# Four waits of a hand-made merge of TensorE's threads, held longer

## The chip, the core and the metric

The program runs on one core of a Trainium2 chip. That core has five engines with a queue of instructions each, worked off in program order: TensorE (PE, with its weight loads listed as PEld), VectorE (DVE), ScalarE (ACT), GpSimd (POOL) and SyncE (SP), which starts most transfers. The metric is the time of one launch on the device in microseconds (us), lower is better.

## The reference

Two blocks of a language model run one after the other over 256 tokens with 16 learned ones ahead (T = 272 columns, 1024 channels). All is float32; the kernel splits each matmul operand into a high and a low part (h, l) and adds three products. The first layer of the first block is a gated delta rule:

```python
proj = h @ w_in                                    # queries, keys, values, z, beta, a
qkv  = silu(conv4(proj[..., :o1]))
beta = sigmoid(proj[..., o2:o3])
g    = -exp(a_log) * softplus(proj[..., o3:] + dt_bias)
q, k = l2_normalize(q), l2_normalize(k)            # per head and token
# per head and chunk of 128 tokens: G = cumsum(g); A = 1 + beta k k^T decay (lower);
# u, w = solve(A, [v beta, k beta exp(G)]); v_new = u - w S; o = q exp(G) S + attn v_new; S = S exp(G_end) + k^T v_new
out  = (rms_norm(o) * silu(z)) @ w_out
```

Behind it come a convolutional feed-forward, an mLSTM layer (queries, keys, values, an output gate, and per head and token two gates whose cumulated log sigmoid weights a 272 x 272 attention), another feed-forward, and the second block (feed-forward, three mixing branches, feed-forward), which the change does not touch.

## The kernel before, in words

TensorE's order is fixed when the program is written; the other engines are ordered by a scheduler that works from it. A small merger, the class Threads, keeps a list of generators ("threads"). Each yields what its next piece on TensorE waits for: tiles, names of PSUM banks, and a number, the *hold*, which is added to the time at which the merger believes the tiles are ready. The merger keeps an estimated clock of TensorE and takes the first thread in its list whose time has come; where none has, it takes the one that comes first and moves its clock up. A hold thus puts no wait into the program: it keeps a thread back, and other threads' pieces are written ahead of it.

In the first layer (`gdn`, names below) the threads are:

- `projections`: four groups of queries, keys, values (`gdn_proj`), and eight slices of z (`gdn_z`). They are matmuls `ps<-xhl,wh` and `ps<-xhl,wl`, always in triples of three matmuls of 272 columns. This thread is last in the list and always ready but for the loads, so its triples are what is put between the pieces of the others: the *filler* below.
- `gdn_gates`: `psba`, `bap`, then the chain of a log sigmoid in tiles `lp` to `gg`, then **`gp`** (sums over time, from `gg`), then the tile `stk`, then `rp` (transposes of `stk`), which gives `rw`. Nothing of a head starts before `rw`.
- `first_chunks`, `second_chunks`: `unit_kq` transposes keys and queries (`kqp<-eye,kv`), scales them to unit length in `kqtok`, and transposes back (**`kqp<-eye,kqtok`**); `gdn_pre` builds the decays (`dp`, `kk`). `second_chunks` also runs `after`, with `gdn_onorm`, which scales the outputs `on` and transposes them (**`otp`**), four times for each of four groups, and then `gdn_tail_pre`.
- four lanes (`gdn_core`): an inverse by doubling (`rtp`, then `yp` and `w` in turn, `zp`, `r2p`), then `up`, `op`, `sp`, `ksp`. Lane 0 ends with `gdn_tail`, the last 16 tokens of all heads: the same inverse, `wp`, `up`, `vnp`, `up`, `rsp`. The product with `w_out` (`ps<-og`) comes after all of it.

In the mLSTM layer `ml_gates` does what `gdn_gates` does: a chain on VectorE to `mlf`, then **`mbp`**, then `mst`, then `mrp`; the filler there is again the projection, and the heads (`ml_head`) wait for `mrp`. The four waits in bold type are those of the change.

Loads: each weight slice of 512 KB is loaded to `wraw` (three buffers), cast by ScalarE to `wh`, and subtracted by GpSimd to `wl` (three buffers each). A slice of the projections serves eight triples.

Of the kernel before, what the change touches and what calls it, by code (L numbers as in the profile page):

```python
# [208 lines left out]
class Kern:  # L209
# [681 lines left out]
    def gdn_gates(self, X):  # L891
        i = self.i
        al, db = self.al, self.db
        self.lane = "u0"
        p = self.plane("psba", (128, T))
        yield from self.row_product(i["gdn_w_in"][0], 6144, 32, X, p)
        ba = self.cst([128, 3, 32], name="ba")
        self.V.memset(ba[:], 0.0)
        gr = self.p_s.tile([32, T], F32, tag="th", name="gr", bufs=2)
        self.A.copy(gr[:], p[:32])  # L900
        yield [gr[:], "pu0"]
        self.lane = "u0"
        p = self.plane("bap", (128, 3, 32))
        for t, (o, P) in enumerate(TT):
            self.tr(p[:P, t, :], gr[:, o:o + P], 32)
        for t, (o, P) in enumerate(TT):
            self.V.tensor_copy(ba[:P, t, :], p[:P, t, :])
        bx, ax = ba[:, :, 0:16], ba[:, :, 16:32]
        self.tt(ax, ax, db[:, None, :].to_broadcast([128, 3, 16]), ALU.add)
        l = self.log1p_exp_neg_abs([128, 3, 32], ba[:])  # L910
        self.act(al[:], al[:], AF.Exp)
        g = self.cst([128, 3, 16], name="gg")
        lb = self.cst([128, 3, 16], name="lb")
        self.stt(g[:], ax, 0.0, l[:, :, 16:32], ALU.max, ALU.add)
        self.stt(g[:], g[:], -1.0, al[:, None, :].to_broadcast([128, 3, 16]), ALU.mult, ALU.mult)
        self.stt(lb[:], bx, 0.0, l[:, :, 0:16], ALU.min, ALU.subtract)
        yield [g[:], "pu0", 1.0]
        self.lane = "u0"
        gp = self.plane("gp", (128, 5, 16))
        for t, (o, P) in enumerate(TT):  # L920
            self.mm(gp[:P, t, :], self.tri[:P, :P], g[:P, t, :])
        for t in range(2):
            self.mm(gp[:, 3 + t, :], self.ones[:], g[:, t, :])
        G = self.cst([128, 3, 16], name="Gc")
        self.V.memset(G[:], 0.0)
        for t, (o, P) in enumerate(TT):
            self.V.tensor_copy(G[:P, t, :], gp[:P, t, :])
        self.nG = self.cst([128, 2, 16], name="nG", tag="ba")
        self.ts(self.nG[:], G[:, 0:2, :], -1.0, ALU.mult)
        self.beta = self.cst([128, 3, 16], name="beta")  # L930
        self.act(self.beta[:], lb[:], AF.Exp)
        self.ts(self.beta[:], self.beta[:], 0.5, ALU.mult)
        Pq = self.cst([128, 3, 16], name="Pq")
        self.tt(Pq[:], G[:], lb[:], ALU.add)
        self.ckt = self.cst([128, 2, 16], name="ckt")
        self.tt(self.ckt[:], gp[:, 3:5, :], G[:, 0:2, :], ALU.subtract)
        self.act(self.ckt[:], self.ckt[:], AF.Exp)
        self.cbg = self.cst([128, 16], name="cbg")
        self.act(self.cbg[:], Pq[:, 1, :], AF.Exp)
        self.ts(self.cbg[:], self.cbg[:], -1.0, ALU.mult)  # L940
        self.eg = self.cst([128, 16], name="eg")
        self.act(self.eg[:], G[:, 1, :], AF.Exp)
        self.gt = self.cst([128, 16], name="gt")
        self.act(self.gt[:], gp[:, 4, :], AF.Exp)
        st = self.cst([128, 3, 96], name="stk")
        hi = self.cst([128, 3, 16], F32R, name="sthi")
        for n, (src, sgn) in enumerate(((Pq, 1.0), (G, 1.0), (G, -1.0))):
            if n < 2:
                self.A.copy(hi[:], src[:])
                self.V.tensor_copy(st[:, :, n * 32:n * 32 + 16], hi[:].bitcast(F32))  # L950
                self.tt(st[:, :, n * 32 + 16:n * 32 + 32], src[:], hi[:].bitcast(F32), ALU.subtract)
        self.ts(st[:, :, 64:96], st[:, :, 32:64], -1.0, ALU.mult)
        yield [st[:], "pu0"]
        self.lane = "u0"
        rp = self.plane("rp", (96, T))
        for t, (o, P) in enumerate(TT):
            self.tr(rp[:, o:o + P], st[:P, t, :], P)
        self.rw = self.cst([96, T], F32R, name="rw")
        self.A.copy(self.rw[:], rp[:])
        xs = self.cst([96, 2, 8, 16], F32R, name="xs")  # L960
        self.tt(xs[:], self.rw[:, None, None, 256:272].bitcast(F32).to_broadcast([96, 2, 8, 16]),
                self.c[:96, CSM:CSM + 16].rearrange("p (e q) -> p e q", e=2)[:, :, :, None].to_broadcast([96, 2, 8, 16]),
                ALU.mult)
        self.xs = xs
# [30 lines left out]
    def unit_kq(self, x, c):  # L995


        n = len(x)
        yield list(x) + [f"pu{c}"]
        self.lane = f"u{c}"  # L1000
        ss = self.tiny([128, n], "kqss")
        p = self.plane("kqp", (128, n, 128))
        for h in range(n):
            self.tr(p[:, h, :], x[h])
        for h in range(n):
            self.square_sum(ss[:, h:h + 1], p[:, h, :])
        r = self.rsqrt_small([128, n], ss[:], 1.0, 4 * EPS)
        rq = r[:].rearrange("p (h e) -> p h e", e=2)[:, :, 1]
        self.ts(rq, rq, 128.0 ** -0.5, ALU.mult)
        kq = self.ring(f"kq{c}", "kqtok", (128, n, 128))  # L1010
        for h in range(n):
            self.act(kq[:, h, :], p[:, h, :], AF.Copy, scale=r[:, h:h + 1])
        yield [kq[:], f"pu{c}", 0.8]
        self.lane = f"u{c}"
        p2 = self.plane("kqp2", (128, n, 128))
        for h in range(n):
            self.tr(p2[:, h, :], kq[:, h, :])
        kqT = self.ring(f"kqT{c}", "kqT", (128, n, 128))
        self.A.copy(kqT[:], p2[:])
        return kq, kqT  # L1020
# [179 lines left out]
    def gdn_onorm(self, on, r, dst):  # L1200

        for h in range(2):
            self.ts(on[:, h, :], on[:, h, :], r[:, h:h + 1], ALU.mult)
        yield [on[:], "pu1", 0.5]
        self.lane = "u1"
        p = self.plane("otp")
        for h in range(2):
            self.tr(p[:, h, :], on[:, h, :])
        self.A.copy(dst, p[:])
# [297 lines left out]
    def ml_gates(self, X, done):  # L1507
# [21 lines left out]
        l = self.log1p_exp_neg_abs([128, 3, 4], ga[:, :, 4:8])  # L1529
        lf = self.cst([128, 3, 4], name="mlf", tag="gg")  # L1530
        self.stt(lf[:], ga[:, :, 4:8], 0.0, l[:], ALU.min, ALU.subtract)
        yield [lf[:], "pb1"]
        bp = self.bank("pb1", (128, 3, 3, 4), "mbp")
        st = self.cst([128, 3, 24], name="mst", tag="stk")
        bs = self.cst([128, 3, 3, 4], name="mbs", tag="lb")
# [915 lines left out]
```

## Time and profile before

| | |
|---|---|
| time, median of 3 runs | 1661.56 us (1658.22 to 1662.08) |
| profiled execution, its own time | 1655.78 us |
| its span, first to last instruction | 1654.0 us |
| TensorE busy | 1547.4 us (94%) |
| VectorE busy | 1124.6 us (68%) |
| ScalarE busy | 929.0 us (56%) |
| GpSimd busy | 581.0 us (35%) |
| mean granted TensorE clock | 0.977 of full |

The table averages over stages with different limits. The first layer runs from about 20 to 366 us of the span and the mLSTM layer from about 655 to 771 us.

### The profile page before, as it was taken

The page shows a single profiled execution, that of the slowest core. Times are in us where ns is not written, and L with a number is a line of the kernel's source. Part 1 is how long each engine was busy: PE and PEld are TensorE (multiplying, and loading weights), DVE is VectorE, ACT ScalarE, POOL GpSimd, SP SyncE. Part 2 cuts the span into 40 slices and gives each one's busy share as a digit, 9 for nine tenths or more (in the row PEclk, how much of TensorE's full clock was granted, in tenths as well). Part 3 has the DMA queues.
Part 4 walks back from the last instruction along what each step waited for, and adds up shares of the span by engine and source line. Part 5 has one row for each costly group of instructions (what it writes and reads, how often), then busy time and mean ns, then how long its engine had stood idle before and what let it go on. Part 6 is the DMA issues. An engine that isn't in the chain of part 4 may idle for free.

```text
span 1654.0 us, 31168 instructions
## 1 busy us (share of the span) xinstructions
PE 1547.4 (94%) x11932; PEld 1461.7 (88%) x11932; DVE 1124.6 (68%) x2231; ACT 929.0 (56%) x1885; POOL 581.0 (35%) x535
## 2 busy tenths in 40 slices
PE   7889888899899999899899999999997899999999
PEld 5778777789799998888799999999986899999987
DVE  6788877757888857357877758665659653566643
ACT  4567667656566645445566645554554664564442
POOL 3674555320200000551143533312265548511221
PEclk9899999999999999999999999999998999999999
DMA  5331221226365553344356665665553435656664
GB/s 160 91 90 52 77 60 45 77 90 196 108 186 187 178 176 112 105 116 133 110 179 190 187 182 156 206 193 176 174 166 106 128 90 156 182 160 192 183 187 153
DMA packets 239099, 235.39 MB, mean 142 GB/s; under 512 B 11510, under 2 KB 226406, under 8 KB 238950
## 3 DMA queue, kind: packets, MB, share of 16 engines
q1 hardware_dynamic: 238326, 231.86, 46.7%
q8 instruction: 94, 1.54, 0.4%
q0 software_dynamic: 496, 1.41, 0.4%
q14 instruction: 55, 0.45, 0.1%
q10 hardware_dynamic: 128, 0.13, 0.0%
HBM read 232.32 MB, written 1.05 MB: 141 GB/s over the span
## 4 chain that ended last, share of the span: by engine, by line
PE 68%; DVE 22%; ACT 5%; DMA 3%; issue 2%; POOL 0%; SPq 0%; ACTq 0%; DVEq 0%; POOLq 0%
PE ps L190 53%; PE pst L190 4%; DVE cy L190 3%; DVE rq_a L190 3%; DVE RT L190 2%; ACT wh L190 2%; DVE wl L190 1%; DVE rq_y L190 1%; DVE xn L190 1%; PE rsp L190 1%; DVE xhl L190 1%; DMA wraw<-in_ffn_w_up_dram 1%; DVE on L190 1%; PE w L190 1%; PE up L190 1%
## 5 line engine op out<-in xcount | busy, mean ns | idle before, releaser
L190 PE MATMUL ps<-xhl,wh 128*128 128x256 f32 (+2 forms) x4496 | 859.6, 293 | 28.2 <-DVE py L190 7.4
L190 PEld LDWEIGHTS ps<-xhl,wh 128*128 128x128 f32 x4496 | 701.4, 192 | 37.9 <-DVE xhl L190 8.0
L190 ACT CAST wh<-wraw 128x1024 fp32r<-128x1024 f32 (+2 forms) x436 | 448.1, 1029 | 382.0 <-PE ps L190 255.7
L190 PE MATMUL ps<-xhl,wl 128*128 128x256 f32 (+2 forms) x2248 | 625.5, 287 | 0.0
L383 POOL TENSOR_TENSOR wl<-wraw,wh 128x512 fp32r<-128x512 f32 (+3 forms) x264 | 336.1, 1297 | 645.1 <-ACT wh L190 597.2
L190 PEld LDWEIGHTS ps<-xhl,wl 128*128 128x128 f32 x2248 | 423.6, 192 | 0.0
L190 DVE TENSOR_TENSOR wl<-wraw,wh 128x1024 fp32r<-128x1024 f32 (+2 forms) x237 | 285.7, 1206 | 166.1 <-ACT wh L190 161.5
L190 POOL TENSOR_TENSOR wl<-wraw,wh 128x512 fp32r<-128x512 f32 x134 | 174.5, 1324 | 150.9 <-ACT wh L190 134.1
L190 PE MATMUL ps<-hh,wh 128*128 128x256 f32 (+1 forms) x1056 | 191.1, 283 | 0.0
L190 PEld LDWEIGHTS ps<-hh,wh 128*128 128x128 f32 x1056 | 163.2, 189 | 0.0
L190 PE MATMUL ps<-hh,wl 128*128 128x256 f32 (+1 forms) x528 | 149.8, 284 | 0.0
L190 DVE SCALAR_TENSOR_TENSOR fy<-ps,pvt,fy 128x256 f32<-128x256 f32 (+2 forms) x176 | 84.9, 488 | 25.7 <-ACT fy L190 23.8
L190 PEld LDWEIGHTS ps<-hh,wl 128*128 128x128 f32 x528 | 99.4, 188 | 0.2 <-DVE wl L190 0.2
L190 DVE SCALAR_TENSOR_TENSOR cy<-cx,pvt,cy 128x271 f32<-128x271 f32 (+2 forms) x96 | 74.4, 778 | 13.7 <-ACT cy L190 12.7
L190 DVE TENSOR_TENSOR hh<-fy,hh 128x256 fp32r<-128x256 f32 (+1 forms) x88 | 66.3, 755 | 14.0 <-ACT hh L190 13.9
L190 POOL MEMSET mvt<- 128x4 f32 x4 | 0.4, 102 | 176.1 <-PE ps L190 176.1
L190 DVE TENSOR_TENSOR py<-ps,rstd 128x256 f32<-128x256 f32 x72 | 30.1, 421 | 38.0 <-PE ps L190 38.0
L190 ACT ACTIVATE fy<-ps,pvt 128x272 f32<-128x272 f32 (+1 forms) x88 | 49.6, 568 | 10.8 <-PE ps L190 10.2
L190 PE MATMUL pst<-wh,hh 128*128 128x512 f32 x176 | 55.1, 394 | 0.0
L190 ACT CAST hh<-fy 128x256 fp32r<-128x256 f32 (+1 forms) x88 | 35.7, 407 | 29.0 <-DVE fy L190 28.4
L190 PE MATMUL ps<-og,wh 128*128 128x272 f32 x256 | 49.5, 291 | 0.1
L190 DVE CAST_PREDICATED RT<-lvl,w 128x512 f16<-128x512 uint8 x67 | 44.9, 684 | 6.7 <-PE w L190 6.3
(521 smaller groups left out, 2400.6 us busy)
## 6 DMA issues: line engine op xcount, KB each, us to landing
wraw<-in_ffn_w_up_dram SPq DMA_DIRECT2D x88, 512.0 KB
wraw<-in_ffn_w_gu_dram SPq DMA_DIRECT2D x88, 512.0 KB
wraw<-in_ffn_w_down_dram SPq DMA_DIRECT2D x79, 512.0 KB
wraw<-in_gdn_w_in_dram SPq DMA_DIRECT2D x48, 512.0 KB
wraw<-in_w_in_dram SPq DMA_DIRECT2D x41, 512.0 KB
wraw<-in_ml_w_in_dram SPq DMA_DIRECT2D x24, 512.0 KB
wraw<-in_gdn_w_out_dram SPq DMA_DIRECT2D x16, 512.0 KB
wraw<-in_mem_w_kv_dram SPq DMA_DIRECT2D x8, 512.0 KB
```

The lines of the kernel that those rows point to most:

```text
L190: r = f(*args, **kw)
L383: eng.tensor_tensor(l[:, a, b], r[:, a, b], h[:, a, b].bitcast(F32), ALU.subtract)
```

## The change

Four numbers: the hold of `gp` goes from 1.0 to 5.0, that of `kqp<-eye,kqtok` from 0.8 to 2.5, that of `otp` from 0.5 to 2.5, and `mbp`, which had none, gets 4.0. No instruction's work changes.

```diff
@@ gdn_gates
         self.stt(lb[:], bx, 0.0, l[:, :, 0:16], ALU.min, ALU.subtract)
-        yield [g[:], "pu0", 1.0]
+        yield [g[:], "pu0", 5.0]
         self.lane = "u0"
         gp = self.plane("gp", (128, 5, 16))
@@ unit_kq
             self.act(kq[:, h, :], p[:, h, :], AF.Copy, scale=r[:, h:h + 1])
-        yield [kq[:], f"pu{c}", 0.8]
+        yield [kq[:], f"pu{c}", 2.5]
         self.lane = f"u{c}"
@@ gdn_onorm
             self.ts(on[:, h, :], on[:, h, :], r[:, h:h + 1], ALU.mult)
-        yield [on[:], "pu1", 0.5]
+        yield [on[:], "pu1", 2.5]
         self.lane = "u1"
@@ ml_gates
         self.stt(lf[:], ga[:, :, 4:8], 0.0, l[:], ALU.min, ALU.subtract)
-        yield [lf[:], "pb1"]
+        yield [lf[:], "pb1", 4.0]
         bp = self.bank("pb1", (128, 3, 3, 4), "mbp")
```

Written anew from the first of them on, TensorE's order differs in the whole first layer and in the mLSTM layer, and nowhere else; SyncE's is the same throughout.

On TensorE, at the gates of the first layer, ahead of `gp` (`trx` are transposes of the residual), the difference begins:

```order
 L190 MATMUL ps<-xhl,wl 128x272
+L190 MATMUL ps<-xhl,wh 128x272 x2
+L190 MATMUL ps<-xhl,wl 128x272
+L190 MATMUL trx<-eye,xt 128x128 x2
+L190 MATMUL trx<-eye,xt 128x16
+L190 MATMUL ps<-xhl,wh 128x272 x2
```

and goes on so: ten triples and three `trx` are put in ahead of `gp`, so that 38 triples of filler come before it, where there were 28. Between `gp` and `rp` stood nine triples and three `trx`; now there are eight triples.

On ScalarE, the same place in the program, from `beta` (the last thing ahead of `gp`'s results) on; before:

```order
L190 ACTIVATE beta<-lb 128x48
L190 ACTIVATE eg<-Gc 128x16
L190 COPY hst<-trx 128x272
L190 ACTIVATE cth<-cy 128x272
L190 ACTIVATE ckt<-ckt 128x32
L190 ACTIVATE gt<-gp 128x16
L190 ACTIVATE cbg<-Pq 128x16
L190 CAST sthi<-Pq 128x48
L190 CAST wh<-wraw 128x1024
```

and now:

```order
L190 ACTIVATE beta<-lb 128x48
L190 CAST wh<-wraw 128x1024
L190 COPY cx<-ps 128x272
L190 ACTIVATE cy<-ps,pvt 128x272
L190 COPY hst<-trx 128x272
L190 ACTIVATE cth<-cy 128x272
L190 COPY hst<-trx 128x272
L190 ACTIVATE cth<-cy 128x272
L190 ACTIVATE eg<-Gc 128x16
L190 CAST wh<-wraw 128x1024
L190 ACTIVATE ckt<-ckt 128x32
L190 ACTIVATE gt<-gp 128x16
```

`sthi` holds the high parts from which `stk`, and so `rp`, is made. Two casts of weights and the copies of a projection moved ahead of it.

On TensorE, the end of the first layer; before, filler stood between all steps of `gdn_tail`, as here, and 16 triples behind its last, `rsp`:

```order
L190 MATMUL ps<-xhl,wl 128x272
L190 MATMUL otp<-eye,on 128x128 x2
L190 MATMUL rsp<-sq,ones 128x256
L190 MATMUL ps<-xhl,wh 128x272 x2
L190 MATMUL ps<-xhl,wl 128x272
```

and now the last steps read:

```order
L190 MATMUL r2p<-RT,Z 128x128
L190 MATMUL wp<-R_5253,kbg 128x128 x2
L190 MATMUL otp<-eye,on 128x128 x2
L190 MATMUL up<-R_5253,bv 128x128 x2
L190 MATMUL up<-wq,St 128x2x16 x16
L190 MATMUL vnp<-eye,vnT 128x128 x2
L190 MATMUL otp<-eye,on 128x128 x2
L190 MATMUL up<-BA,vn 128x128 x2
L190 MATMUL rsp<-sq,ones 128x256
L190 MATMUL ps<-og,wh 128x272 x2
```

The filler has moved up: from the start of lane 0's last inverse (its `rtp`) to `ps<-og` there were 63 triples, now 20, and none of them is behind that inverse's last `yp`. In the mLSTM layer 28 triples now stand between `mgp`, the transposes ahead of the gates' chain, and `mbp`, where there were 16, and eight instead of six between `mbp` and `mrp`.

## Rows read from the trace of the kernel before

**Rows 1.** By stretch: length; busy PE, PEld, DVE, ACT, POOL; clock; transfers' share, GB/s.
```profile
20.00:366.00 346.00, 296.42 (x2447) 270.89 (x2448) 264.68 (x631) 220.50 (x663) 180.99 (x196) 0.95 0.26 75
655.00:771.00 116.00, 107.38 (x775) 95.68 (x773) 64.08 (x173) 53.45 (x121) 55.74 (x46) 0.97 0.39 111
```
**Rows 2.** What TensorE waited for from 20 to 380: us in total, times, longest.
```profile
PE yp L190 <- DVE RT L190: 14.4, 11, 3.3
PE kqp L190 <- ACT kqtok L190: 6.7, 4, 3.5
PE gp L190 <- DVE gg L190: 5.3, 1, 5.3
PE otp L190 <- DVE on L190: 5.0, 3, 4.4
...
PE ps L190 <- DVE zs L190: 3.8, 3, 2.0
```

**Rows 3.** TensorE in order of time, around `gp` (start, us, idle before).
```profile
32.37 0.41 PE L190 MATMUL ps<-xhl,wh 128*128 128x272 f32 x2
...
32.75 0.42 PE L190 MATMUL ps<-xhl,wh 128*128 128x272 f32 x2
...
41.05 1.20 PE L190 MATMUL gp<-gg,cc 128*128 128x16 f32 x6 [5.32 <-DVE gg L190]
...
45.51 0.65 PE L190 MATMUL ps<-xhl,wh 128*128 128x272 f32 x2
...
46.19 0.65 PE L190 MATMUL ps<-xhl,wh 128*128 128x272 f32 x2
...
51.52 0.54 PE L190 MATMUL rp<-eye,stk 128*96 128x128 f32 x3 [0.46 <-DVE stk L190]
```

**Rows 4.** TensorE in order of time, at the longest waits of `kqp` and `otp`.
```profile
77.43 1.12 PE L190 MATMUL kqp<-eye,kqtok 128*128 128x128 f32 x4 [3.54 <-ACT kqtok L190]
...
195.48 0.66 PE L190 MATMUL kqp<-eye,kqtok 128*128 128x128 f32 x4 [1.77 <-ACT kqtok L190]
...
234.77 0.69 PE L190 MATMUL otp<-eye,on 128*128 128x128 f32 x2 [4.36 <-DVE on L190]
```

**Rows 5.** The same columns for the stretches behind four of these waits.
```profile
41.00:50.00 9.00, 8.95 (x40) 7.97 (x40) 4.14 (x18) 3.63 (x13) 1.96 (x2) 0.54 0.23 61
...
77.00:83.00 6.00, 5.57 (x23) 4.98 (x24) 4.88 (x8) 4.92 (x15) 3.62 (x3) 0.50 0.07 7
...
234.00:240.00 6.00, 5.23 (x30) 4.73 (x31) 4.51 (x15) 1.84 (x5) 1.52 (x2) 0.50 0.29 87
...
674.00:681.00 7.00, 7.00 (x41) 6.60 (x41) 2.29 (x17) 1.27 (x2) 0.00 (x0) 0.52 0.21 71
```

**Rows 6.** The mLSTM gates in order of time, TensorE and VectorE.
```profile
673.82 0.59 PE L190 MATMUL mbp<-mlf,cc 128*128 128x4 f32 x2 [4.98 <-DVE mlf L190]
...
680.55 0.55 PE L190 MATMUL mrp<-eye,mst 128*24 128x128 f32 x3
...
677.23 0.17 DVE L190 TENSOR_TENSOR mst<-mbs,mhi 128x36 f32<-128x36 f32 x1
```

**Rows 7.** ScalarE's cast for `stk`, and GpSimd's queue at `mrp`.
```profile
48.80 0.25 ACT L190 CAST sthi<-Gc 128x48 fp32r<-128x48 f32 x1
...
681.41 0.74 POOL L190 DMA_DIRECT2D qkw<-in_mla_q_norm_dram  x1 [8.90 <-PE mrp L190]
682.17 2.54 POOL L190 TENSOR_TENSOR wl<-wraw,wh 128x512 fp32r<-128x512 f32 x2
```

**Rows 8.** TensorE in order of time, the end of the first layer.
```profile
332.61 0.28 PE L190 MATMUL yp<-RT,Br 128*128 128x128 f16 x2
...
334.30 0.28 PE L190 MATMUL w<-Y,RT 128*128 128x128 f16 x2
...
358.98 0.60 PE L190 MATMUL rsp<-sq,ones 128*128 128x256 f32 x2
...
366.20 0.56 PE L190 MATMUL ps<-og,wh 128*128 128x272 f32 x2
```

## The prediction

> **What bounds the kernel now.** I read four views. The stretches give the layer: from 20 to 366 TensorE is busy 296.4 of 346 us, so it stands still for 50 us; in the mLSTM layer for 8.6 of 116; VectorE is busy 76% of the first layer [rows 1]. TensorE is therefore what sets the time, wherever it waits for nothing, and the change can only move its idle time and its clock. The list of waits says for whom it waits: 14.4 us in the inverse (`yp` for `RT`), which the change does not name, and 6.7, 5.3 and 5.0 us at `kqp`, `gp` and `otp` [rows 2]. In order of time one sees that `gp`'s is one wait of 5.32 us [rows 3], that the largest at `kqp` are 3.54 and 1.77 us and one of 4.36 us makes up `otp`'s [rows 4], and that `mbp` waits 4.98 us [rows 6]. These 22 us are the places of the change. Behind them the granted clock stands at or near one half, 1.2 GHz in place of 2.4, for 9, 6, 6 and 7 us [rows 5]: a triple then takes 0.68 us (45.51 to 46.19), where it took 0.38 (32.37 to 32.75) [rows 3].
>
> **What a hold can do.** It makes no filler. The triples that now cover a wait are taken from behind, where they covered others. So each edit has a gain at its place, and all share one price where filler runs out.
>
> *mbp.* 12 more triples stand ahead of it, 12 x 0.38 = 4.5 us against a wait of 4.98 [rows 6]. Then the clock should not fall: from 674 to 681 TensorE was busy 7.0 us at 0.52 [rows 5], which at full clock is some 3.6 us, 3.4 less. The next wait is `mrp`, with eight triples ahead (3.0 us); `mst` was written 1.1 us after `mbp`'s last matmul (the filler begins again at about 676.3; `mst` at 677.23 [rows 6]), so it is covered. The slices are there: the filler that moves up is that of the next two slices, and on GpSimd one more subtraction now stands ahead of the transfer `qkw`, which waits for `mrp` [rows 7], not behind it. Gain 4.5 + 3.4, less 0.4 for small waits: 7.5 us; between 4.5 (the clock falls all the same) and 8.4.
>
> *gp.* Ten triples, 3.8 us, and three `trx` now stand ahead of it, against 5.32: the wait goes. But what is late next is `rp`, which took its 51.52 from a chain over VectorE and ScalarE, not from TensorE: `gp` starts when `gg` is done, at 41.05 as before, and ScalarE's cast of `sthi` came at 48.80 [rows 3, 7]. Two casts of weights and a projection's copies now stand ahead of `sthi` on ScalarE, while the copies do not wait any more for triples at half clock. I put `rp` at about 50. TensorE reaches it at about 45.7 (`gp` and its sums some 1.6 us at full clock, eight triples 3.0), and waits some 4 us more. It is then eleven triples ahead of where it was at 50, 4.1 us, and loses about 1 of it to the clock that falls again there: gain 3 us. Lower bound 0 (`rp` as late as before plus the casts, 52 to 53); upper 8.5, when `rp` needs no wait: 5.3 of wait and 3.2 of clock, the ten triples at 0.68.
>
> A rule bears on this one. GpSimd did not start a subtraction whose cast was long done until the transfer in front of it had got its `mrp`, 8.90 us later, and began it at 682.17, right behind [rows 7]. The Trainium skill, page "TensorE: Matmul & The Clock Gate", section "Architectural detail: the array is 16× 32×32, not 1× 128×128", says that ScalarE and VectorE take their queues strictly in order, and each of GpSimd's cores its own. By that rule the casts ahead of `sthi` delay `rp`, and the edit gives 3; if they could be passed, 8.5, and the sum below would be 5.5 us better.
>
> *kqp and otp.* Holds are 1.7 and 2.0 us longer, and so much more filler goes ahead of each. At `kqp` that takes 1.7 of 3.54, 1.7 of 1.77, and the other two waits, together 6.7 - 3.54 - 1.77 = 1.4: 4.8 us. At `otp` it takes 2.0 of 4.36 and the rest, 0.6: 2.6 us. The clock behind them cost half of 5.57 and of 5.23 us of busy time [rows 5], 2.8 and 2.6; since waits of about 2 us stay, I give back half, 2.7. Together 10 us. Lower bound 0: VectorE, at 76%, is late at both places because its queue is full, and filler that comes earlier brings it more work first. Upper: 11.7 of waits and 5.4 of clock, 17.
>
> *The end.* Here the filler is missing. From the start of lane 0's last inverse, 63 triples were left, 16 of them behind `rsp`; now 20 are left, none behind the last `yp`. I price each step that has nothing beside it. From a `yp` to its `w` 1.69 us passed, with triples all the way and no wait [rows 8], so a bare one is no more; I take 1.4 for each of `yp` to `w`, `zp` to `r2p`, `r2p` to `wp`, 1.2 from `w` to `zp` and 1.0 from `wp` to `up` (an `otp` stands between), 0.5 for one step that is half covered, and 1.6 for the three short ones from `up` to `rsp`: 8.5 us. Behind `rsp`, 358.98 + 0.60, the first `ps<-og` came at 366.20, 6.6 us later [rows 8], all under filler; now bare. Sum 15.1. Against that go the three waits of `ps` for `zs`, 3.8 us [rows 2], which all lie in this stretch, as the filler that waited has gone. Then the clock: it will fall in 15 us of such gaps, and `ps<-og` begins at half; I take 1.5 net, as it was already low for some of this stretch. Price 12.8 us; between 7 (ScalarE, with no casts to do, is quick behind `rsp`, and steps take 1.0) and 18 (the clock also stretches `up` and the first 6 us of `ps<-og`).
>
> **Sum.** 7.5 + 3 + 10 - 12.8 = 7.7 us less, on the profiled execution's own 1655.8 us (1654.0 of span and 1.8 around it): 1648. That execution is 5.8 us below the median of the runs shown, and the same difference from the median gives 1661.6 - 7.7 = 1654. A measurement of this kernel tells a difference of about 0.3%, 5 us, from none.
>
> **Rivals.**
>
> *The filler stays where it pays.* The four waits and their clock come back nearly whole and the end is quick: 8 + 6 + 14 - 9 = 19 us less, 1643. For it: all four waits are long and single, with the filler ready. Against it: `rp` and VectorE's 76%.
>
> *The waits only move.* TensorE gets ahead and then stands at the next tile of VectorE, as it did for 14.4 us at `yp` already [rows 2]. Then the first layer gives 5 in place of 13, the end takes 12.8 and the mLSTM layer gives 7.5: no change, 1661 to 1662.
>
> *The end decides, slower.* `second_chunks` is one thread, and it now carries sixteen `otp` and four `kqp` that are held 2.0 and 1.7 us longer. If these holds lengthen its chain by more than the filler ahead of it saves, the last inverse begins later and bare: from `rtp` to `ps<-og` some 30 us with 15 of them idle at a low clock. With 18 at the end, 0 to 3 gained in the first layer and 7.5 in the other, 7 to 10 us more: 1670. It decides from the point at which the end costs 5 us more than both layers give back: 12.5 us where the first gives nothing. For it: the tail's start moved back by a hundred places in TensorE's order, and 43 triples (16 us) went ahead of it. Against it: 11.7 us of waits that were there to be filled.
>
> That the change does nothing is out: the orders differ.
>
> **How the numbers follow.** The forecast (1 to 13 us less) gets 0.42, the first rival 0.20, the second 0.18, the last 0.20. Of the forecast's 0.42, 0.30 lie beyond 5 us; the first rival adds 0.20: faster 0.50. The rest of the forecast, 0.12, and 0.15 of the second rival make 0.27 for no difference; the last rival and the rest, 0.23, slower. The range leaves out half of each outer rival: from 20 us less to 10 more, 1641 to 1672. The forecast's own range is 1648 to 1661.
>
> **What would show it.** In the new profile: no wait at `gp`, and one of 3 to 5 us at `rp` near 50; `mbp` without a wait of over 0.6 us and a full clock from 674 to 681 of the old time; `kqp` and `otp` together under 5 us; from the last triple of the first layer to `ps<-og` 12 to 16 us of idle TensorE, half of it behind `rsp`. I am wrong if the idle time between 20 us and the last inverse does not fall by some 10 us, or if the end is covered by something that the order does not show.

## The result, and the profile after

The changed kernel takes 1681.43 us (median of 4 runs, 1677.13 to 1683.14), the kernel before 1660.20 (4 runs): a ratio of 1.0128, 95% interval 1.0106 to 1.0150, so 21.2 us slower, where 8 us less was forecast. The profiled execution took 1677.13 us, 21.35 more than that of before.

By stretches, in the columns of [rows 1]: the first layer, the same cut where the filler ends, and the mLSTM layer.

```profile
20.00:384.10 364.10, 304.88 (x2449) 277.89 (x2449) 267.72 (x638) 227.29 (x669) 180.24 (x196) 0.92 0.26 74
20.00:360.90 340.90, 290.06 (x2384) 265.82 (x2385) 260.85 (x621) 218.03 (x652) 180.24 (x196) 0.94 0.27 76
360.90:384.10 23.20, 14.83 (x67) 12.07 (x64) 6.87 (x17) 9.26 (x18) 0.00 (x0) 0.56 0.14 45
...
675.00:792.00 117.00, 109.15 (x782) 96.53 (x780) 60.89 (x175) 54.38 (x123) 55.72 (x46) 0.97 0.39 110
```

`ps<-og` comes at 384.06 instead of 366.20, so the first layer is 17.9 us longer: 9.6 more of idle TensorE (364.1 - 304.9 = 59.2 against 49.6 [rows 1]) and 8.3 more of the same work at a lower clock. Up to the last triple TensorE stood still for 50.8 us: the waits that were to be filled are gone, and as much idle time is there as in the whole layer before. The mLSTM layer is no shorter: from `mgp` to the last `mtp` 107 us pass in both kernels. Of the remaining 3.5 us, some 1.8 are the clock at the start of `ps<-og` (a granted clock of 0.69 in its first 6 us, full before); the rest is spread.

What TensorE waited for from 20 to 398 (us in total, times, longest):

```profile
PE yp L190 <- DVE RT L190: 24.9, 14, 5.3
PE zp L190 <- DVE RT L190: 7.8, 7, 1.8
PE ps L190 <- ACT cy L190: 7.0, 3, 4.2
PE rp L190 <- DVE stk L190: 3.6, 1, 3.6
PE ps L190 <- ACT og L190: 3.3, 1, 3.3
```

`gp`, `kqp` and `otp`, 17 us in [rows 2], are not in the list any more. `yp` has 10.5 us more, `zp` 3.1, `ps` for `cy` 5.6, and `rp` 3.1.

VectorE's last step for `gp`, then TensorE in order of time: the gates, the first and last `otp` of the first group, the last one of the second and third, lane 0's last `rtp`, and the end of the layer.

```profile
41.40 0.20 DVE L190 SCALAR_TENSOR_TENSOR gg<-gg,al 128x48 f32<-128x48 f32 x1
...
44.31 0.65 PE L190 MATMUL gp<-gg,cc 128*128 128x16 f32 x6
...
52.27 0.54 PE L190 MATMUL rp<-eye,stk 128*96 128x128 f32 x3 [3.65 <-DVE stk L190]
...
172.06 0.38 PE L190 MATMUL otp<-eye,on 128*128 128x128 f32 x2
...
199.61 0.39 PE L190 MATMUL otp<-eye,on 128*128 128x128 f32 x2
...
270.50 0.38 PE L190 MATMUL otp<-eye,on 128*128 128x128 f32 x2
...
326.17 0.39 PE L190 MATMUL otp<-eye,on 128*128 128x128 f32 x2
...
348.17 0.27 PE L190 MATMUL rtp<-identh,RT 128*128 128x128 f16 x2
...
360.59 0.29 PE L190 MATMUL ps<-xhl,wl 128*128 128x272 f32 x1
360.72 0.28 PE L190 MATMUL yp<-RT,Br 128*128 128x128 f16 x2
362.50 0.27 PE L190 MATMUL w<-Y,RT 128*128 128x128 f16 x2 [1.49 <-ACT Y L190]
...
368.85 6.88 PE L190 MATMUL up<-wq,St 128*128 128x32 f32 x32
...
379.51 1.22 PE L190 MATMUL rsp<-sq,ones 128*128 128x256 f32 x2 [0.96 <-ACT sq L190]
384.06 1.12 PE L190 MATMUL ps<-og,wh 128*128 128x272 f32 x2 [3.33 <-ACT og L190]
```

The same `otp` and `rtp`, and `up` over the states, in the kernel before:

```profile
170.43 0.28 PE L190 MATMUL otp<-eye,on 128*128 128x128 f32 x1
...
184.15 0.39 PE L190 MATMUL otp<-eye,on 128*128 128x128 f32 x2
...
248.42 0.39 PE L190 MATMUL otp<-eye,on 128*128 128x128 f32 x2
...
299.85 0.39 PE L190 MATMUL otp<-eye,on 128*128 128x128 f32 x2
...
321.08 0.28 PE L190 MATMUL rtp<-identh,RT 128*128 128x128 f16 x2
...
349.19 3.66 PE L190 MATMUL up<-wq,St 128*128 128x32 f32 x32
```

Up to lane 0's last `rtp`, in the columns of [rows 1]: before, then after.

```profile
20.00:321.08 301.08, 256.81 (x2141) 232.87 (x2142) 239.47 (x568) 197.84 (x608) 166.61 (x186) 0.95 0.26 73
```

```profile
20.00:348.17 328.17, 279.98 (x2304) 256.62 (x2305) 251.06 (x591) 212.31 (x636) 179.48 (x196) 0.94 0.27 76
```

The first group's four `otp` take 27.6 us from first to last, where they took 13.7. The last `otp` of the three groups comes 15.5, 22.1 and 26.3 us later, lane 0's last `rtp` 27.1 later. From there on the layer is quicker, 35.9 us instead of 45.1, as nothing stands between the steps; but from the last triple on the granted clock is 0.56, and `up` over the states takes 6.88 us, where it took 3.66. The idle time up to that `rtp` is 48.2 us, where it was 44.3: it rose by 3.9.

The mLSTM gates: after, TensorE's `mbp`, the seven equal steps of the log sigmoid on VectorE (one row by tile: least, median and longest in ns, first and last start), and GpSimd beside them; then the last two for before.

```profile
697.56 0.39 PE L190 MATMUL mbp<-mlf,cc 128*128 128x4 f32 x2 [4.45 <-DVE mlf L190]
...
L190 DVE SCALAR_TENSOR_TENSOR lp_p<-lp_p,lp_q x7: 1182/1218/1242, 688.4 to 695.9; 128x12 f32<-128x12 f32 x7
...
687.05 10.02 POOL L190 TENSOR_TENSOR wl<-wraw,wh 128x512 fp32r<-128x512 f32 x8 [0.72 <-ACT wh L190]
```

```profile
L190 DVE SCALAR_TENSOR_TENSOR lp_p<-lp_p,lp_q x7: 170/171/1186, 668.9 to 673.2; 128x12 f32<-128x12 f32 x7
...
667.55 4.96 POOL L190 TENSOR_TENSOR wl<-wraw,wh 128x512 fp32r<-128x512 f32 x4 [0.72 <-ACT wh L190]
```

The filler was there and `mbp` still waited: the twelve triples bring four more subtractions on GpSimd, and a VectorE step takes 0.17 us alone and 1.2 us beside one. Now all seven steps have one beside them, where three had.

### The profile page after: what moved, and what is told of

Its sections match the earlier page's. It is cut to its first block, busy times and chain, and to the rows that moved or that the text cites. A ratio compares the mean times of both kernels' runs of the same rounds, so it can differ in the third digit from the quotient of the medians.

```text
span 1675.3 us, 31155 instructions
## 1 busy us (share of the span) xinstructions
PE 1556.4 (93%) x11932; PEld 1469.0 (88%) x11932; DVE 1121.4 (67%) x2231; ACT 932.9 (56%) x1885; POOL 578.0 (35%) x535
## 4 chain that ended last, share of the span: by engine, by line
PE 41%; DVE 8%; ACT 2%; DMA 1%; issue 1%; POOL 0%; ACTq 0%; POOLq 0%; DVEq 0%
PE ps L190 34%; PE pst L190 5%; DVE rq_a L190 1%; ACT wh L190 1%; DVE rq_y L190 1%; DVE wl L190 1%; DVE qtok L190 1%; DMA wraw<-in_ml_w_out_dram 0%; DMA wraw<-in_ffn_w_up_dram 0%; DVE qsq L190 0%; PE rsp L190 0%; POOL wl L383 0%; PE scp L190 0%; DVE smx L190 0%; PE memp L190 0%
## 5 line engine op out<-in xcount | busy, mean ns | idle before, releaser
L190 DVE SCALAR_TENSOR_TENSOR cy<-cx,pvt,cy 128x271 f32<-128x271 f32 (+2 forms) x96 | 69.8, 728 | 14.2 <-ACT cy L190 11.7
L190 ACT ACTIVATE fy<-ps,pvt 128x272 f32<-128x272 f32 (+1 forms) x88 | 49.6, 568 | 10.3 <-PE ps L190 9.8
L190 PE MATMUL ps<-og,wh 128*128 128x272 f32 x256 | 50.8, 297 | 3.3 <-ACT og L190 3.3
```

Source lines behind the costliest of these rows:

```text
L190: r = f(*args, **kw)
```

## The experiments

All are timed against the kernel before on the same chip; "us" is the difference of the medians. It and the ratio are two estimates and differ by up to 3 us (e10, e14, e16).

| run | what differs from the kernel before | us | ratio (95%) |
|---|---|---|---|
| e1 | `gp` held 5.0 | -3.1 | 0.9986 (0.9965 to 1.0008) |
| e2 | `kqp` held 2.5 | +9.2 | 1.0068 (1.0045 to 1.0090) |
| e3 | `otp` held 2.5 | +8.3 | 1.0051 (1.0034 to 1.0068) |
| e4 | `mbp` held 4.0 | -0.7 | 0.9992 (0.9979 to 1.0005) |
| e5 | `otp` held 2.5 in the first group only | +11.3 | 1.0063 (1.0044 to 1.0083) |
| e6 | `otp` held 2.5 in the last group only | +2.2 | 1.0021 (1.0003 to 1.0040) |
| e7 | `mbp` held 4.0, GpSimd's work in eighths (mLSTM) | -4.2 | 0.9974 (0.9958 to 0.9990) |
| e8 | GpSimd's work in eighths, both layers | -23.4 | 0.9864 (0.9840 to 0.9888) |
| e9 | `kqp` and `otp` held 2.5 | +21.3 | 1.0139 (1.0113 to 1.0165) |
| e10 | `kqp` and `otp` not held | +5.3 | 1.0046 (1.0027 to 1.0065) |
| e11 | all four edits and eighths | +5.8 | 1.0045 (1.0027 to 1.0063) |
| e12 | `gp` 5.0, `mbp` 4.0 and eighths | -22.7 | 0.9875 (0.9849 to 0.9901) |
| e13 | all four edits and 24 more triples | +16.9 | 1.0106 (1.0082 to 1.0129) |
| e14 | 24 more triples | +14.3 | 1.0071 (1.0054 to 1.0089) |
| e15 | GpSimd's work in quarters, both layers | -7.4 | 0.9950 (0.9929 to 0.9971) |
| e16 | GpSimd's work in eighths (mLSTM) | -5.2 | 0.9951 (0.9933 to 0.9968) |
| e17 | e7 and `rang` as a product of two tensors | -4.1 | 0.9977 (0.9963 to 0.9991) |
| e18 | e12 and the same for `rang` | -23.7 | 0.9868 (0.9845 to 0.9891) |

**Each edit alone (e1 to e4), and the two together (e9).** Each has one line of the change's diff, e9 two.

> Only the hold of gp is raised, 1.0 to 5.0; from rp on TensorE's order is that of the kernel before, with nine triples moved ahead. The theory (the loss comes from the two holds of second_chunks, kqp and otp, which spread that thread's pieces and use up the filler before the end): 2 to 4 us less, since in the changed kernel rp came 0.8 us later with nine triples (3.4 us) more ahead of it, and 63 triples are still left for the last inverse. The rival (filler that moves up at the gates brings VectorE's and GpSimd's work forward, and the whole of the layer behind runs late): 3 to 8 us more.

> Only the hold of kqp is raised, 0.8 to 2.5. In TensorE's order 49 triples are left from lane 0's last rtp (63 before, 20 with all four edits) and none behind rsp. The theory (second_chunks is the chain that ends last, and every hold on it makes it longer): 3 to 8 us more, most of it between the last rtp and ps<-og, with otp alone worse. The rival (the waits at kqp were idle time of TensorE and are filled): 3 to 6 us less.

> Only the hold of otp is raised, 0.5 to 2.5: sixteen places on second_chunks. 45 triples are left from the last rtp, none behind rsp. The theory: 6 to 14 us more, the largest part of the change; the four otp of one group take over 20 us from the first to the last in the first group, as in the changed kernel (27.5 us; 13.8 before). The rival (only kqp and otp together use the filler up): within 4 us of the kernel before.

> Only mbp is held, by 4.0; TensorE's order differs in the mLSTM layer alone. The theory (the filler that covers the wait brings four more subtractions on GpSimd, and an operation of VectorE with two tensors in SBUF does not run beside one: the seven steps of the log sigmoid take 8.7 us in the changed kernel, 4.4 before): mbp still waits 4 to 5 us, and the kernel takes 0 to 3 us more. The rival (VectorE was late there only because of what the first layer left behind): mbp's wait is under 1 us, and 4 to 8 us less.

> The longer holds of kqp and otp together, those of gp and mbp as before. The theory (these two carry the whole loss, and gp and mbp give back a little): their single costs, 9 to 11 and 8 us, add up, 17 to 25 us more, so at least as much as all four edits together (21). The rival (the loss needs gp's or mbp's edit beside them): under 15 us more.

`kqp` and `otp` each cost 8 to 9 us alone, and together as much as the whole change. That `otp` would be the larger part was not borne out. `gp`'s edit is not told from none; its sign is that of the forecast. `mbp`'s does nothing that can be told from none, with the same wait as after:

```profile
677.73 0.59 PE L190 MATMUL mbp<-mlf,cc 128*128 128x4 f32 x2 [4.60 <-DVE mlf L190]
```

So VectorE's lateness there is no legacy of the first layer.

**Where on the thread (e5, e6).**

```diff
-                yield from self.gdn_onorm(on[g, n], r[:, n, :], ...)
+                yield from self.gdn_onorm(on[g, n], r[:, n, :], ...,
+                                          2.5 if g == 0 else 0.5)
```

(e6: `g == 3`.)

> The longer hold (2.5) is on otp in the first of the four groups alone, 0.5 in the others. The theory (second_chunks is one chain, so a delay early in it is carried on to the end, and the filler spent on it is missing there): four places of sixteen already cost about half of what all sixteen did, 3 to 6 us more; lane 0's last rtp comes 5 us or more later than in the kernel before (321.08). In TensorE's order 54 triples are left from there and 6 behind rsp. The rival (each hold costs at its own place, alike): a quarter, 2 us more.

> The longer hold is on otp in the last group alone. All before lane 0's last rtp is as in the kernel before, and 63 triples are left from there, 14 of them behind rsp. The theory (a hold costs by what it delays behind it and by the filler it uses): almost nothing stands behind these four, so within 3 us of the kernel before. The rival (the end of the layer, where little filler is left, is where the holds hurt): 4 us more or above.

TensorE in e5, in order of time: the last `otp` of groups one to three, lane 0's last `rtp`, and `ps<-og`.

```profile
195.71 0.38 PE L190 MATMUL otp<-eye,on 128*128 128x128 f32 x2
...
247.87 0.39 PE L190 MATMUL otp<-eye,on 128*128 128x128 f32 x2
...
305.37 0.39 PE L190 MATMUL otp<-eye,on 128*128 128x128 f32 x2
...
331.04 0.28 PE L190 MATMUL rtp<-identh,RT 128*128 128x128 f16 x2
...
375.65 0.82 PE L190 MATMUL ps<-og,wh 128*128 128x272 f32 x2 [2.42 <-ACT og L190]
```

Four holds of sixteen, the first four, cost about as much as all sixteen (the intervals overlap), where I expected half; the last four cost little. The delay is 11.6 us at the first group's last `otp`, nothing at the second's, 5.5 at the third's, and 10.0 at the last `rtp`; `ps<-og` comes 9.4 later. So it isn't handed on from `otp` to `otp`. In the code two things stand behind the first group's scaling: the inverses of the third group, which wait for it (`after_done`), and the rest of `second_chunks`, next the third group's `kqp` for the second chunk. The third group's `kqp` of `second_chunks` and its first and last inverse, before and in e5:

```profile
201.99 0.66 PE L190 MATMUL kqp<-eye,kqtok 128*128 128x128 f32 x4 [0.66 <-ACT kqtok L190]
...
208.66 0.28 PE L190 MATMUL rtp<-identh,RT 128*128 128x128 f16 x2
...
224.97 0.28 PE L190 MATMUL rtp<-identh,RT 128*128 128x128 f16 x2
```

```profile
208.66 0.28 PE L190 MATMUL rtp<-identh,RT 128*128 128x128 f16 x2
...
209.94 0.60 PE L190 MATMUL kqp<-eye,kqtok 128*128 128x128 f32 x4
...
232.76 0.42 PE L190 MATMUL rtp<-identh,RT 128*128 128x128 f16 x2
```

The first inverse begins at 208.66 in both, 13 us behind the first group's last `otp` in e5, so `after_done` does not hold it. The `kqp` comes 8.0 us later and the last inverse 7.8: in this trace the rest of `second_chunks` carries the delay, past the second group, whose inverses had begun before, to the third. No run took the two apart. At the end of e5 almost nothing is bare, that is, without filler beside it (2.4 us of wait at `ps<-og`): the loss does not need the filler to run out.

**The other direction (e10).** Both holds set to 0.

> The other direction: the holds of kqp and otp are both 0. In TensorE's order 71 triples are left from lane 0's last rtp (63 before) and 27 behind rsp (16). If what counts is that second_chunks comes early, the kernel takes 2 to 6 us less, though TensorE then waits longer at kqp and otp themselves (11.7 us before). If the holds of before stand near their best, the waits at these places outweigh it and it takes 2 to 8 us more.

Shorter is slower too: `kqp` and `otp` now wait 10.8 and 7.0 us. That an earlier `second_chunks` is always better is refuted. The holds of before stand between two costs.

**Is TensorE the limit at the end (e13, e14)?**

```diff
+            p = self.ps()
+            h, l = self.hl
+            for n in range(24):
+                xh, xl = X[4 + n % 4]
+                yield [xl]
+                self.mm(p[:], h[:, n % 4, 0:128], xh, n == 0, False)
+                self.mm(p[:], h[:, n % 4, 0:128], xl, False, False)
+                self.mm(p[:], l[:, n % 4, 0:128], xh, False, n == 23)
```

It stands at the end of `projections`; `self.hl` is the last slice of z.

> The changed kernel with 24 triples more behind the last slice of z: they repeat products of that slice, into a bank that nobody reads, and can be put between the steps of the last inverse, which stand bare. They are 9.1 us of TensorE's work at full clock. The theory (the end of the layer is set by the chain of second_chunks and lane 0, which comes too late, and TensorE has time there): they cost nothing or give a little back, as the clock falls less; 15 to 23 us above the kernel before, where the changed kernel is 21 above. The rival (TensorE's work sets the end there too): 28 to 31 above.

> The same 24 triples in the kernel before. Both theories: TensorE stood still nowhere between lane 0's last rtp and ps<-og but for small waits, so they cost their whole time, 8 to 11 us more.

From lane 0's last `rtp` to `ps<-og`, by stretch: the changed kernel, and with the extra triples.

```profile
348.17:384.06 35.89, 24.87 (x146) 21.23 (x143) 16.62 (x47) 14.94 (x33) 0.75 (x1) 0.72 0.19 59
```

```profile
348.77:385.84 37.07, 28.36 (x219) 26.50 (x216) 16.73 (x47) 14.97 (x33) 0.74 (x1) 0.89 0.18 57
```

The 24 triples are 72 matmuls, 9.1 us of work at full clock. In the changed kernel 73 more matmuls take 1.2 us more there, at a clock of 0.89 in place of 0.72; the whole kernel is no slower (16.9 above before, against 21.2). In the kernel before the same triples cost 14.3 us (between 9 and 15 by the ratio), more than the 8 to 11 expected: beside their own work, TensorE's waits for `zs` grew from 3.8 to 6.4 us. So after the change the end is set by the chain, with TensorE free beside it, and before by TensorE.

**VectorE beside GpSimd (e7, e8, e11, e12, e15, e16).** A slice's subtraction, two instructions of 512 columns, is cut into eight of 128 (e15: four of 256); TensorE's order stays, as the merger is still told of two. `self.cut` is 8 (4) in the layers named and 2 elsewhere.

```diff
-            eng, pieces = self.nc.gpsimd if self.ordered or self.mixing else self.G, 2
+            eng, pieces = self.nc.gpsimd if self.ordered or self.mixing else self.G, self.cut
```

> mbp is held by 4.0 as in the changed kernel, and GpSimd's subtractions in the mLSTM layer are cut into eight instructions a slice in place of two; TensorE's order is that of the run with mbp's hold alone. The theory (each small VectorE operation waits for the end of the GpSimd instruction that runs): the seven steps, 8.4 us with instructions of 1.27 us, take 3 to 4.5 us; mbp waits under 1 us; 3 to 6 us less than the kernel before. The rival (the two engines share a bandwidth, or GpSimd's work as such delays VectorE): the seven steps still take 7 us or more.

> The four holds are those of the kernel before, TensorE's order too; GpSimd's subtractions are cut into eight instructions a slice in both layers. If VectorE's waits for the end of a GpSimd instruction are what makes its tiles late in the first layer (gg, kqtok, on, RT), the waits of TensorE there shrink and the kernel takes 5 to 15 us less; if VectorE is late there because it has that much work, it stays within 3 us.

> All four longer holds, and GpSimd's subtractions cut into eight instructions a slice in both layers. The theory (the holds' cost is in the order of second_chunks, apart from VectorE's waits for GpSimd): it stays 14 to 24 us above the kernel with the cut alone, so about where the kernel before is, and mbp waits under 1 us. The rival (the holds cost because the filler they put ahead brings GpSimd's work in VectorE's way): most of the loss goes, within 8 us of the kernel with the cut alone.

> The cut in both layers with the longer holds of gp and mbp, and those of kqp and otp as before: the two edits that gained a little, on the kernel that gained most. 22 to 28 us less than the kernel before if they add to the cut's 23; 18 to 22 less if the cut has already taken away the waits that they cover (gp waited 4.6 us with the cut, mbp 0.6).

> Subtractions of GpSimd in four instructions a slice in both layers (256 columns each), holds as before. The theory (a VectorE operation waits for the end of the GpSimd instruction that runs): the seven steps in the mLSTM layer take 0.6 to 0.75 us each, between the 1.2 of two instructions a slice and the 0.38 of eight; 12 to 22 us less than the kernel before. The rival (a threshold in the length): as with eight.

> The cut into eight in the mLSTM layer alone, mbp not held. With it the two layers' shares of the 23 us come apart: by the trace of the cut in both layers, mbp waited 0.6 us and the stretch from mgp to the last mtp took 7.7 us less; so 5 to 9 us less. If the longer hold of mbp were still good for something beside the cut, this would be slower than the run with both (4.3 less).

The seven steps by tile with eighths (e7) and with quarters (e15):

```profile
L190 DVE SCALAR_TENSOR_TENSOR lp_p<-lp_p,lp_q x7: 378/384/390, 669.6 to 672.1; 128x12 f32<-128x12 f32 x7
```

```profile
L190 DVE SCALAR_TENSOR_TENSOR lp_p<-lp_p,lp_q x7: 645/649/662, 664.5 to 668.6; 128x12 f32<-128x12 f32 x7
```

A step takes 1.22, 0.65 and 0.38 us as GpSimd's instruction is 1.30, 0.74 and 0.46 us long (medians by tile), and 0.17 alone: it waits for the instruction that runs, and over these three lengths the delay goes with the length. The Trainium skill, page "SBUF — State Buffer", section "Who interferes with whom", says that a VectorE instruction with two inputs in SBUF contends with a GpSimd one that reads SBUF, over ports that one of them holds for its whole instruction. These rows agree, and a share of a bandwidth would not shorten with the cut.

In e7 `mbp` waits no more, but the kernel gains only 4.2 us, and the cut without the hold (e16) gains 5.2 (8 by the ratio): once VectorE is quick, the hold shows no gain. In the first layer the cut does what no hold did. Stretch of e8's first layer, in the same columns:

```profile
20.00:357.59 337.59, 296.37 (x2450) 272.28 (x2450) 247.82 (x633) 222.01 (x665) 229.14 (x472) 0.94 0.27 77
```

Idle TensorE falls to 41.2 us, from 49.6 [rows 1], and VectorE's busy time by 17, with as many instructions; so part of its 76% was waiting. (That execution, 1646.43 us, is the slowest of e8's five, median 1638.42.) In e18, which has the longer hold of `gp` beside the cut and whose profiled execution, 1635.16 us, lies at its median, idle TensorE falls to 32.8 us:

```profile
20.00:345.72 325.72, 292.93 (x2448) 269.05 (x2449) 243.44 (x632) 220.34 (x664) 230.17 (x472) 0.96 0.28 80
```

Quarters gave 7 where I expected 12 to 22: a step's time falls by two thirds of what eighths take off it, the kernel's by a third, and why is not known. e11 against e8 shows that the four longer holds cost 29 us with the cut as well: their loss is not VectorE's waiting for GpSimd. e12 and e18, 23 to 24 us below the kernel before, are not told from e8: no gain of the longer holds of `gp` and `mbp` shows beside the cut's.

**What holds `mrp` (e17, e18).** In e7 the wait moved to `mrp`. VectorE, GpSimd and TensorE there, in order of time:

```profile
678.98 6.00 DVE L190 TENSOR_SCALAR rang<-cc,posf 128x16 f32<-128x16 f32 x1
...
664.22 20.73 POOL L385 TENSOR_TENSOR wl<-wraw,wh 128x128 fp32r<-128x128 f32 x48 [27.04 <-ACT wh L190]
...
685.68 0.49 PE L190 MATMUL mrp<-eye,mst 128*24 128x128 f32 x3 [3.77 <-DVE mst L190]
```

```diff
-            self.ts(a[:, t, :], self.c[:, CINV:CINV + 16], pf[:, t:t + 1], ALU.mult)
+            self.tt(a[:, t, :], self.c[:, CINV:CINV + 16], pf[:, t:t + 1].to_broadcast([128, 16]), ALU.mult)
```

> The run with mbp's hold and eight instructions a slice in the mLSTM layer, where mrp waited 3.77 us because one VectorE operation of 16 columns ahead of mst (rang, a product of a table with a scalar) took 6.00 us beside GpSimd's work. Here that product is written as an operation on two tensors, the form that got in after one GpSimd instruction in the seven steps. The theory (that form waits for one instruction, the other for the end of the whole train of them): rang takes under 0.5 us, mrp does not wait, 2 to 4 us less than the run without it, 6 to 9 less than the kernel before. The rival (rang was held by something else): it still takes 5 us or more, and the time stays.

> The same on the fastest kernel so far (the cut in both layers, gp's and mbp's longer holds, 20.8 us less by its ratio; there rang took 6.0 us too). The theory: 2 to 4 us less than that, 22 to 26 less than the kernel before; the rival: no change.

In e17, VectorE:

```profile
676.46 6.03 DVE L190 TENSOR_TENSOR rang<-cc,posf 128x16 f32<-128x16 f32 x1
```

`rang` takes 6 us in either form, `mrp` waits 3.75 us, and the time is the same. My theory of the two forms fell. Both times `rang` ends with the last of GpSimd's instructions, 664.22 + 20.73 = 684.95 in e7; why it waits for all of them and the seven steps for one each stays open.

## Why the prediction was wrong

- **kqp and otp, the failed step.** "Together 10 us" of gain, "lower bound 0". Their waits did go, all 11.7 us, and the two edits cost 21.3 us (e9), of which the end is some 17 (below; in e9 too 23.2 us pass from the last triple to `ps<-og`). I took a hold as a choice between two places for the same filler, with one price at the end, and did not count what it delays: a group's `otp` come one behind the other, so a hold is paid four times in a row, and the later chunks on the same thread wait for the group. In the changed kernel the last `rtp` is 27.1 us later. The 43 triples that moved ahead of it are 16.3 of that (at 0.38), and the other 34 of the 163 matmuls more, the other lanes' last pieces, some 4.5 (an estimate from their spacing in the kernel before). That leaves some 6 us lost, 3.9 of idle time and the rest clock, where I had put 13 less; that the idle time up to the last inverse would not fall by some 10 us was the sign named for being wrong. e5 shows the price with almost no bare end.
- **mbp, the second failed step.** "Gain 7.5, between 4.5 and 8.4": measured 0.7, not told from none, and `mbp` waits 4.45 us, where I allowed 0.6. I took `mlf`'s time as fixed. The covering triples need subtractions on GpSimd, and these slow the chain that they cover. "`mrp` covered" held until the chain was made quick (e7).
- **gp.** The signs were right: no wait at `gp`, 3.65 us at `rp`. Gain 3 forecast and 3.1 measured, though the interval reaches from 5.8 of gain to 1.3 of loss, so it is not told from none. The way there was another, and the match is in part luck: I had `gp` start at 41.05 as before, but the filler ran 2.7 us past the end of `gg` (41.60) and `gp` came at 44.31; from it to `rp` 8.0 us passed in place of 10.5, so `rp` came at 52.27, not 50.
- **The end.** The sum of idle time and clock was right and its parts were not. From the last triple to `ps<-og` 23.2 us pass, with 14.83 us of work at a clock of 0.56, some 8.3 at full clock, so 14.9 us are lost, and 1.8 in the first 6 us of `ps<-og`. I had 15.1 of idle time and 1.5 of clock; it is 8.4 of idle time and 6.5 + 1.8 of clock, so that 16.7 met 16.6 was luck. The steps up to `rsp` stood idle for 5.0 us, not 8.5. Behind `rsp` 3.3 us passed, not 6.6: those 6.6 in the kernel before were the time of the 16 triples there (6.1) and a wait for `zs` of 0.5, not that of the chain.
- **Sum.** From 7.7 less to 21.2 more are 29 us: about 7 from `mbp`, some 16 from `kqp` and `otp` ahead of the last triple (340.9 us up to it, where the same work took 366.2 - 20 - 8.3 = 337.9 before, so 3.0 more in place of 13 less), 4 from the end, in which I had set 3.8 us of waits for `zs` against the price (2.3 of them stayed), and the rest behind the layer.
- **The rivals.** The last one named the thread and the sign, and gave 1670; it too rested on the filler running out at the end and on 7.5 us from `mbp`. "The waits only move" is what happened up to the last triple.

## What to carry to other kernels

Before a wait is filled, ask what stands behind it on its own thread: a short wait of TensorE on a chain that others wait for can be cheaper than more filler, and here a delay early in the chain cost more than one late in it (11 us against 2). Holds of 0 were dearer too (e10). Filler isn't free for the other engines: look at what it makes GpSimd and VectorE do while the awaited tile is being made, op by op, and take a small operation's own time from a place where its neighbour is idle. Where small VectorE steps stretch beside long GpSimd instructions, cut those: here that gave 23 us in eighths and 7 in quarters, with TensorE's order unchanged.

## What the runs showed of the hardware

A VectorE step of 12 columns took 0.17 us alone and 0.38, 0.65 or 1.22 us beside GpSimd instructions of 0.46, 0.74 or 1.30 us; the profile counts the wait as busy time. One of 16 columns took 6.00 us beside some 14 such instructions (20.73 us / 48 = 0.43 each), until the last had ended. And filler kept the clock up: with 24 more triples the same end of the layer had a granted clock of 0.89 in place of 0.72.
